# A fused two-block kernel: another order of the 32-, 64- and 128-slot positions in its first mixture of experts

## The chip, the cores and the metric

The kernel runs on one core of a Trainium2 chip. The metric is the device time of one execution in microseconds, the median of several runs. The engines that matter here are TensorE (PE, with its weight loads PEld), VectorE (DVE), ScalarE (ACT), GpSimdE (POOL) and SyncE (SP), whose queue issues nearly all transfers from HBM.

## The reference, cut to what matters

Two transformer blocks are computed for 256 tokens of width 1024, in fp32. The change concerns the first mixture of experts, which sits in the middle of the first block:

```python
logits = hf @ w_router + b_router           # 256 tokens, 32 experts
top_v, top_e = lax.top_k(logits, 4)         # 4 experts for each token
gates = jax.nn.softmax(top_v, axis=-1)
# for each expert e, over the tokens that chose it:
hc = xi @ w1[e] + b1[e]                     # w1[e]: 1024 x 2048
g, u = hc[:, :1024], hc[:, 1024:]
g, u = jnp.minimum(g, 7.0), jnp.clip(u, -7.0, 7.0)
hm = (u + 1.0) * (g * jax.nn.sigmoid(1.702 * g))
yb = hm @ w2[e] + b2[e]                     # w2[e]: 1024 x 1024
# y[token] += gate * yb
```

Each expert's weights are 12 MB of fp32 (8 MB for `w1`, 4 MB for `w2`) and 384 MB for all 32.

## The kernel before

The mixture runs through 32 *positions*, one expert each. A position has a fixed size: 32 slots ("s"), 64 ("m") or 128 ("b", done as two chunks of 64). A slot holds one token. Positions 0 and 1 always hold experts 0 and 1; at run time the other experts are ranked by how many tokens they have, and the ranks are dealt to positions so that larger experts get larger positions (`RANK1`). There are 2 b, 16 m and 14 s. Tokens beyond a position's slots would go to a loop after the positions; with these inputs that loop makes no pass.

For every position the kernel does, in this order:

1. **Loads.** Twelve transfers of 1 MB on SP's queue: eight of `w1` (`in_wei`) and four of `w2` (`in_weo`). From position 2 on SP first reads the expert's number from `oi` (L1106).
2. **First product** (L956 for s, L962 for m and b): for each of the eight `w1` tiles, products of the gathered tokens `xg` with the tile, accumulated in PSUM tiles `h`. An s packs four 32-column products side by side, an m or b two 64-column ones.
3. **Activation**: `h` is copied to `hs` (L973), turned by TensorE (L976), and DVE and ACT make `hm` of it (L979 to L985).
4. **Second product** (L997): `hm` with the four `w2` tiles into PSUM tiles `s`.
5. **Scatter**: `ys` and its two halves (L1010 to L1012), the slot mask (L1005, L1007), products with the mask (L1027), and the sum into `xres` (L1030). It runs beside the next position.

Tokens are gathered for groups of positions with up to 128 slots together (L1050 and L910), ahead of their use. After position 8 the kernel adds the second biases and counts the extra chunks once (L935, L943, L833 to L842).

All weights go through a ring of 17 tiles of 1 MB, `turn % 17`. A load can be issued once the last product that read the tile 17 loads earlier is done. SP's queue is strictly in order, and so is TensorE's; which position's products follow which on TensorE is set when the program is built, by a planner with costs of its own, so two neighbouring positions can be interleaved. The lines on which the change acts:

```python
RING1 = "mmrmrmrmrmrmrmrmm"
def ring_tile():
    turn[0] += 1
    if more_ring:
        pool, order = more_ring
        i = turn[0] % len(order)
todo = [(p, c) for p in range(NE1) for c in CHK1[p]]
for p in range(NE1):
    while (p, CHK1[p][-1]) not in ready or ...:
        gather_on(8)
    er = nc.sync.value_load(route.oi[0:1, p:p + 1], min_val=0, max_val=NE1 - 1)
    expert1(w1, w2, [ready[p, c] for c in CHK1[p]], lambda: places(p), ...)
```

Of the kernel before, what the change touches and what calls it, by code (L numbers as in the profile page):

```python
# [24 lines left out]

NE1, CAP1 = 32, 64
FIX1 = 2
SIZE1 = "mm" + "smsmsbsmsmmsmsmsmsbsmsmmsmsmms"
ROOM1 = [{"b": 128, "m": 64, "s": 32}[c] for c in SIZE1]
CHK1 = [[(o, min(CAP1, r)) for o in range(0, r, CAP1)] for r in ROOM1]  # L30
RANK1 = list(range(FIX1)) + [0] * (NE1 - FIX1)
for _r, _p in enumerate(sorted(range(FIX1, NE1), key=lambda p: -ROOM1[p])):
    RANK1[_p] = FIX1 + _r
assert len(SIZE1) == NE1

# [1837 lines left out]
```

## Time and profile before

| | |
|---|---|
| median of 3 runs | 2324.02 us (2322.54 to 2326.08) |
| the profiled execution | 2327.09 us, span 2325.3 us |
| PE busy | 2158.1 us, 93% of the span |
| DVE busy | 1126.3 us, 48% |
| ACT busy | 785.4 us, 34% |
| mean DMA rate over the span | 300 GB/s |

Busy shares are averages over stages with different limits; the mixture with the 32 positions takes from about 250 to 1235 us of the span. Times in the rows below are microseconds from the start of the span; GB/s is what the core's sixteen DMA engines moved.

### The profile page before, as it was taken

What the parts mean: (1) busy time and instruction counts of PE and PEld (TensorE: products, weight loads), DVE (VectorE), ACT (ScalarE), POOL (GpSimd) and SP (SyncE); (2) the same over time, 40 slices, a digit from 0 to 9 for tenths busy, and PEclk for the clock granted to TensorE, in tenths of its full rate; (3) what the DMA queues carried; (4) which work ended last, traced back from release to release, by engine and by line L of the source; (5) the groups of instructions that cost most, each with busy time, mean ns of one, the idle gap of its engine ahead of it and who ended that gap; (6) DMA issues with size and microseconds to landing.
All of it is one profiled execution on the core that took longest, in us unless ns stands there. A gap on an engine that the chain in (4) does not pass through costs nothing. (4 is left out here: it accounts for less than half of the span.)

```text
span 2325.3 us, 34078 instructions
## 1 busy us (share of the span) xinstructions
PE 2158.1 (93%) x13530; PEld 1424.9 (61%) x13530; DVE 1126.3 (48%) x2048; ACT 785.4 (34%) x1313; POOL 34.9 (2%) x45
## 2 busy tenths in 40 slices
PE   6999999899999889998797999999999899999996
PEld 4888533333333333333235988998888788777983
DVE  3976222323322322322236657654665775337883
ACT  3354211101111111111104655444465564335771
POOL 0000000000000000000000010000001000000000
PEclk9999899998999989999897999999999989999998
DMA  9757689998999999999898334555533467779884
GB/s 395 282 217 271 242 321 417 416 407 344 410 416 416 416 416 412 415 415 416 367 416 335 134 109 164 182 189 183 188 130 110 166 223 275 281 298 349 330 329 197
DMA packets 122630, 697.52 MB, mean 300 GB/s; under 512 B 11120, under 2 KB 11648, under 8 KB 63936
## 3 DMA queue, kind: packets, MB, share of 16 engines
q1 hardware_dynamic: 121120, 690.54, 76.1%
q0 software_dynamic: 1344, 4.73, 0.7%
q8 instruction: 109, 1.79, 0.3%
q14 instruction: 57, 0.47, 0.1%
HBM read 694.18 MB, written 1.05 MB: 299 GB/s over the span
## 5 line engine op out<-in xcount | busy, mean ns | idle before, releaser
L328 DVE TENSOR_TENSOR wl<-w,wh 128x1024 fp32r<-128x1024 f32 (+1 forms) x393 | 476.9, 1223 | 256.7 <-ACT wh L325 247.5
L325 ACT CAST wh<-w 128x1024 fp32r<-128x1024 f32 (+1 forms) x393 | 407.4, 1044 | 304.5 <-PE acc L306 65.7
L962 PE MATMUL h<-w,xg 128*64 128x512 f32 x1280 | 302.0, 620 | 0.0
L997 PE MATMUL s<-w,hm 128*64 128x512 f32 (+1 forms) x1088 | 252.1, 651 | 17.6 <-DVE hm L985 14.1
L962 PEld LDWEIGHTS h<-w,xg 128*64 128x64 f32 x1280 | 93.7, 142 | 186.7 <-issue 182.2
L306 PE MATMUL acc<-xTl,wh 128*128 128x256 f32 x528 | 149.7, 284 | 0.0
L305 PE MATMUL acc<-xTh,wh 128*128 128x256 f32 x528 | 149.7, 283 | 0.0
L307 PE MATMUL acc<-xTh,wl 128*128 128x256 f32 x528 | 149.6, 283 | 0.0
L973 ACT COPY hs<-h 128x512 f32<-128x512 f32 x34 | 19.9, 585 | 373.2 <-PE h L962 290.5
L997 PEld LDWEIGHTS s<-w,hm 128*64 128x64 f32 (+1 forms) x1088 | 62.2, 132 | 130.8 <-issue 95.0
L956 PE MATMUL h<-w,xg 128*32 128x512 f32 x896 | 114.4, 635 | 17.6 <-DMA w<-in_wei 17.6
L973 DVE COPY hs<-h 128x512 f32<-128x512 f32 x20 | 13.8, 691 | 235.9 <-PE h L962 235.9
L910 PEld LDWEIGHTS t<-oh,xh 128*128 128x128 f32 x512 | 70.5, 209 | 76.2 <-ACT xg L911 32.2
L911 ACT ACTIVATE xg<-t,modc,a 128x128 f32<-128x128 f32 (+3 forms) x128 | 55.4, 440 | 182.2 <-PE t L910 126.4
L307 PEld LDWEIGHTS acc<-xTh,wl 128*128 128x128 f32 x528 | 99.3, 188 | 4.2 <-issue 3.1
L305 PEld LDWEIGHTS acc<-xTh,wh 128*128 128x128 f32 x528 | 99.3, 188 | 2.5 <-issue 1.5
L306 PEld LDWEIGHTS acc<-xTl,wh 128*128 128x128 f32 x528 | 99.3, 188 | 2.0 <-issue 1.1
L306 PE MATMUL f<-fxl,wh 128*128 128x256 f32 x352 | 99.9, 284 | 0.0
L305 PE MATMUL f<-fxh,wh 128*128 128x256 f32 x352 | 98.9, 282 | 0.7 <-ACT fxh L1236 0.7
L307 PE MATMUL f<-fxh,wl 128*128 128x256 f32 x352 | 99.3, 283 | 0.0
L910 PE MATMUL t<-oh,xh 128*128 128x128 f32 (+3 forms) x512 | 85.5, 309 | 14.2 <-ACT xg L911 7.1
L1011 ACT CAST ysh<-ys 128x512 fp32r<-128x512 f32 x34 | 21.0, 618 | 222.6 <-DVE ys L1010 207.4
(540 smaller groups left out, 4294.8 us busy)
## 6 DMA issues: line engine op xcount, KB each, us to landing
w<-in_wei SPq DMA_DIRECT2D x256, 1024.0 KB, 18.4
w<-in_weo SPq DMA_DIRECT2D x128, 1024.0 KB, 19.9
w<-in_wm SPq DMA_DIRECT2D x128, 1024.0 KB, 5.8
w<-in_wf SPq DMA_DIRECT2D x33, 1024.0 KB, 4.8
w<-in_w2in SPq DMA_DIRECT2D x32, 1024.0 KB, 5.1
w<-in_wada SPq DMA_DIRECT2D x24, 1024.0 KB, 9.7
w<-in_win SPq DMA_DIRECT2D x16, 1024.0 KB, 8.6
w<-in_w2out SPq DMA_DIRECT2D x8, 1024.0 KB, 4.9
```

The source lines that it names most:

```text
L305: T.matmul(o, l[0], r[0], start=start, stop=False)
L306: T.matmul(o, l[0], r[1], start=False, stop=False)
L307: return T.matmul(o, l[1], r[0], start=False, stop=stop)
L325: A.copy(wh[:, :m], w[:, o:o + m])
L328: V.tensor_sub(wl[:, :m], w[:, o:o + m], wh[:, :m])
L910: T.matmul(pt[:, 0:n], xh2[:, tt, k * P:(k + 1) * P], oh[:, tt, 0:n], start=tt == 0, stop=tt == 1)
L911: taken.append(A.activation(xg[:, k, 0:n], pt[:, 0:n], AF.Identity, bias=sh2[:, k:k + 1], scale=a2[:, k:k + 1]))
L956: T.matmul(ph[0][0][32 * q:32 * q + 32, :].rearrange("p (i c) -> p i c", i=4), chunks[0][:, k], w5[:, q % 2, q // 2], start=k == 0, stop=k ...
L962: T.matmul(p[j][64 * gu:64 * gu + 64, :], xs[:, k], w[:, gu * D + j * 512:gu * D + j * 512 + 512], start=k == 0, stop=k == 7)
L973: (A.copy if j == 0 else V.tensor_copy)(hs[:, j], p[j])
L997: T.matmul(p[r, :], hm[:, kk * 2 + k], w[:, k * D + hf * 512:k * D + hf * 512 + 512], start=kk == 0 and (small or k == 0), stop=kk == 3 an ...
L1011: A.copy(yp[0], ys)
```

## The change

One string is written in another order; nothing else differs. The first two positions stay "mm".

```diff
-SIZE1 = "mm" + "smsmsbsmsmmsmsmsmsbsmsmmsmsmms"
+SIZE1 = "mm" + "ssssmbssmmsmmsmbsssmmmsmmsmmms"
```

Both strings hold the same letters: 14 s, 14 m and 2 b. Position 7 is a b in both; the second b moves from position 20 to 17. The rest of the table (`ROOM1`, `CHK1`, `RANK1`) follows from the string. There are 16 gather groups before and after, and SP issues the same number of loads in the same sequence of ring tiles.

The first difference is on DVE, in the masks `oh` by which the first groups are gathered (`oh_2689` is the group that begins with position 1, `oh_2853` and `oh_2855` the one after it):

```order
 L1050 TENSOR_SCALAR oh_2689<-ca,posm_2601 128x64 x2
-L1050 TENSOR_SCALAR oh_2689<-ca,posm_2601 128x32 x2
-L1050 TENSOR_SCALAR oh_2853<-ca,posm_2601 128x64 x2
-L1050 TENSOR_SCALAR oh_2853<-ca,posm_2601 128x32 x2
+L1050 TENSOR_SCALAR oh_2689<-ca,posm_2601 128x32 x4
+L1050 TENSOR_SCALAR oh_2855<-ca,posm_2601 128x32 x4
+L1050 TENSOR_SCALAR oh_2855<-ca,posm_2601 128x64 x2
```

The first group was position 1 (64) and 2 (32) and is now 1, 2 and 3; the next was 3 (64) and 4 (32) and is now 4, 5 (32 each) and 6 (64).

On TensorE, the end of position 8's second product (an s in both) and the start of position 9's first one. Before (`h_4142` and `h_4143` belong to position 9):

```order
L943 MATMUL t_4107<-beo,gT 128x512
L997 MATMUL s_4056<-w_4075,hm_4005 32x512 x4
L833 MATMUL t_4110<-cnt_2542,perm_2541 32x1
L1027 MATMUL s_4220<-ysh_4087,gt_4084 128x512
L841 MATMUL t_4119<-ca,more_4113 128x32
L842 MATMUL t_4119<-ca,more_4113 128x32
L1027 MATMUL s_4228<-ysh_4087,gt_4084 128x512
L962 MATMUL h_4142<-w_4144,xg_3825 64x512 x2
L962 MATMUL h_4143<-w_4144,xg_3825 64x512 x2
```

Of the change, at the same place (`h_4111` belongs to position 9):

```order
L997 MATMUL s_4025<-w_4044,hm_3980 32x512 x4
L943 MATMUL t_4076<-beo,gT 128x512
L833 MATMUL t_4079<-cnt_2542,perm_2541 32x1
L1027 MATMUL s_4176<-ysh_4056,gt_4053 128x512
L1027 MATMUL s_4184<-ysh_4056,gt_4053 128x512
L1027 MATMUL s_4176<-ysl_4057,gt_4053 128x512
L956 MATMUL h_4111<-w_4112,xg_3438 32x512 x4
L1027 MATMUL s_4184<-ysl_4057,gt_4053 128x512
L841 MATMUL t_4088<-ca,more_4082 128x32
```

The work that is done once after position 8 stays in its place; what follows it is an s now, and was an m.

On TensorE again, positions 27 (m) and 28 (s) of before. `h_6992` and `h_6993` are position 27's first product, `h_7147` position 28's, and `hs_7042` is position 27's copy that the activation starts from. The rows are the last two of position 27's first product, the last four of position 28's, and what follows:

```order
L962 MATMUL h_6992<-w_7036,xg_6320 64x512 x2
L962 MATMUL h_6993<-w_7036,xg_6320 64x512 x2
...
L956 MATMUL h_7147<-w_7172,xg_6320 32x512 x4
L956 MATMUL h_7147<-w_7178,xg_6320 32x512 x4
L956 MATMUL h_7147<-w_7184,xg_6320 32x512 x4
L956 MATMUL h_7147<-w_7190,xg_6320 32x512 x4
L910 MATMUL t_6939<-oh_6927,xh_2417 128x32 x2
L910 MATMUL t_6943<-oh_6927,xh_2417 128x32 x2
L1005 MATMUL t_6972<-cz,posm_2601 128x128 x2
L976 MATMUL t_7047<-cz,hs_7042 128x128 x4
```

Of the change, positions 27 (s, second product into `s_7073`) and 28 (m, first product into `h_7118` and `h_7119`, copy `hs_7168`):

```order
L997 MATMUL s_7073<-w_7086,hm_7024 32x512 x4
L997 MATMUL s_7073<-w_7092,hm_7024 32x512 x4
L962 MATMUL h_7118<-w_7120,xg_6448 64x512 x2
L962 MATMUL h_7119<-w_7120,xg_6448 64x512 x2
...
L962 MATMUL h_7118<-w_7162,xg_6448 64x512 x2
L962 MATMUL h_7119<-w_7162,xg_6448 64x512 x2
L910 MATMUL t_7065<-oh_7053,xh_2417 128x32 x2
L910 MATMUL t_7069<-oh_7053,xh_2417 128x32 x2
L1005 MATMUL t_7098<-cz,posm_2601 128x128 x2
L976 MATMUL t_7173<-cz,hs_7168 128x128 x4
```

Before, the whole first product of position 28 stood between position 27's first product and the turning of its result, so position 27's second product came after both. In the changed program no position stands between the first and the second product of another; a position's first product does stand directly behind the second product of the one before, ahead of the gather, mask and scatter work of that one, at 5 to 6, 9 to 10, 11 to 12, 13 to 14, 15 to 16, 19 to 20, 21 to 22, 23 to 24, 25 to 26 and 27 to 28. Before, that was so at 14 to 15, 16 to 17, 18 to 19, 22 to 23, 24 to 25 and 26 to 27.

## Rows read from the trace of the kernel before

**Rows 1.** The page: GB/s in 40 slices of the span, each 58 us.

```profile
GB/s 395 282 217 271 242 321 417 416 407 344 410 416 416 416 416 412 415 415 416 367 416 335 134 109 164 182 189 183 188 130 110 166 223 275 281 298 349 330 329 197
```

**Rows 2.** Windows of the mixture; the last column is the DMA rate.

```profile
core 0: us, PE busy (x) PEld busy (x) DVE busy (x) ACT busy (x) POOL busy (x), PEclk, DMA share, GB/s
340.00:367.00 27.00, 24.07 (x144) 9.50 (x144) 8.96 (x19) 3.35 (x7) 0.00 (x0) 0.87 1.01 400
367.00:516.00 149.00, 136.55 (x706) 51.52 (x703) 41.75 (x94) 18.87 (x40) 0.00 (x0) 0.98 1.02 415
516.00:605.00 89.00, 82.67 (x420) 31.01 (x416) 28.96 (x65) 11.20 (x23) 0.00 (x0) 0.92 0.92 361
605.00:1138.00 533.00, 476.02 (x2406) 178.37 (x2406) 148.05 (x318) 63.24 (x135) 0.00 (x0) 0.93 1.01 415
1110.00:1117.00 7.00, 5.32 (x28) 0.61 (x24) 0.00 (x0) 0.00 (x0) 0.00 (x0) 0.50 1.02 422
1138.00:1160.00 22.00, 21.64 (x120) 8.62 (x122) 8.14 (x15) 3.16 (x7) 0.00 (x0) 1.00 0.73 300
367.00:1235.00 868.00, 783.05 (x3964) 291.91 (x3960) 249.82 (x538) 101.41 (x215) 0.00 (x0) 0.94 1.00 406
```

**Rows 3.** The page: DMA issues, with the median us to landing.

```profile
w<-in_wei SPq DMA_DIRECT2D x256, 1024.0 KB, 18.4
w<-in_weo SPq DMA_DIRECT2D x128, 1024.0 KB, 19.9
w<-in_wf SPq DMA_DIRECT2D x33, 1024.0 KB, 4.8
```

**Rows 4.** Timeline of SP: first issue and length, positions 5, 7, 7, 8, 20, 29.

```profile
378.40 22.60 SPq L247 DMA_DIRECT2D w<-in_wei  x8
...
437.62 17.94 SPq L247 DMA_DIRECT2D w<-in_wei  x8
457.73 10.18 SPq L247 DMA_DIRECT2D w<-in_weo  x4
...
468.75 17.27 SPq L247 DMA_DIRECT2D w<-in_wei  x8
...
864.42 9.76 SPq L247 DMA_DIRECT2D w<-in_weo  x4
...
1118.54 29.94 SPq L247 DMA_DIRECT2D w<-in_wei  x8
```

**Rows 5.** Timeline of PE at positions 2, 7, 7, 8, 9, 10, 11, 12, 20, 31.

```profile
340.28 1.06 PE L956 MATMUL h<-w,xg 128*32 128x512 f32 x8
...
471.03 27.69 PE L962 MATMUL h<-w,xg 128*64 128x512 f32 x128
...
513.63 10.51 PE L997 MATMUL s<-w,hm 128*64 128x512 f32 x44
...
524.71 1.90 PE L956 MATMUL h<-w,xg 128*32 128x512 f32 x10
...
559.23 3.68 PE L962 MATMUL h<-w,xg 128*64 128x512 f32 x8
...
594.84 1.06 PE L956 MATMUL h<-w,xg 128*32 128x512 f32 x8
...
616.90 13.95 PE L962 MATMUL h<-w,xg 128*64 128x512 f32 x64
...
647.70 1.94 PE L962 MATMUL h<-w,xg 128*64 128x512 f32 x8
...
917.07 10.51 PE L997 MATMUL s<-w,hm 128*64 128x512 f32 x44
...
1222.30 1.06 PE L956 MATMUL h<-w,xg 128*32 128x512 f32 x8 [1.27 <-DMA w<-in_wei]
```

**Rows 6.** Timeline of PE where position 28's first product and 27's second begin.

```profile
1108.42 1.94 PE L956 MATMUL h<-w,xg 128*32 128x512 f32 x8 [7.01 <-DMA w<-in_wei]
...
1134.46 1.12 PE L997 MATMUL s<-w,hm 128*64 128x512 f32 x2 [1.74 <-DVE xres L1030]
```

## The prediction

> **What bounds the kernel now.** I read the DMA rate over the whole span first, then windows of the mixture, then the order of time on SP and on TensorE. The page's GB/s line stands at 407 to 416 from the seventh slice on and stays there until the mixture ends, with dips to 344 and 367 [rows 1]. Everywhere else it is far lower. So the mixture's loads run at a ceiling of 416 GB/s, and one load of 1 MB takes 1048576 B / 416 GB/s = 2.52 us, the twelve of a position 30.2 us. Summed over 367 to 1235 us the rate is 406 [rows 2]: the loads lost 868 x (1 - 406/416) = 20.9 us against the ceiling. Two windows hold nearly all of it: 516 to 605 with 361 GB/s, 89 x (1 - 361/416) = 11.8 us, and 1138 to 1160 with 300, 22 x (1 - 300/416) = 6.1 us, together 17.9; the 533 us between them ran at 415 and lost 1.3 [rows 2]. TensorE had work that is as long: from the starts of positions 7, 8, 10, 11 and 12 on PE, a b takes 524.71 - 471.03 = 53.7 us, an s 616.90 - 594.84 = 22.1, an m 647.70 - 616.90 = 30.8 [rows 5]. So an s gives back 8.1 us against the loads, an m loses 0.6, a b loses 23.5. At the end of the mixture it is the loads that TensorE waits for: the last tile of position 31's first product came after a wait of 1.27 us on DMA [rows 5]. What moves the last load therefore moves the end, and what TensorE wins by itself does not.
>
> **When the DMA engines run dry.** A ring tile is loaded again 17 loads later, at full rate 17 x 2.52 = 42.8 us after its own issue. With the queue full a load lands 18.4 to 19.9 us after its issue, an undisturbed one after 4.8 [rows 3], so the reissue can be some 15 us late before the engines are empty. A tile must thus be read within about 42.8 + 15 = 57.8 us of its issue; I call the time from issue to last reading its age. Two places test this. Position 7, the first b, issued its four `w2` loads from 457.73 on, the last at about 465.3 (three loads of 2.52 later) [rows 4], and read the last tile until 513.63 + 10.51 = 524.1 [rows 5]: age 58.8, over the limit, and the rate falls from 516 on [rows 2]. The second b, position 20, issued its last at 864.42 + 7.6 = 872.0 [rows 4] and read it until 917.07 + 10.51 = 927.6 [rows 5]: age 55.6, under the limit, and there the window shows no loss [rows 2]. The first loss grew after the b: position 8 took 559.23 - 524.71 = 34.5 us instead of 22.1 [rows 5], since the second biases and the count of extra chunks are done there, and an m followed it while the ring was already full. The other loss has another cause. Position 28's first product had to wait 7.01 us for its first tile at 1108.42 and was paced by its loads, and position 27's second product, which stood behind it in TensorE's order, began at 1134.46 [rows 6]; so four tiles of position 27 were held, and SP needed 29.94 us for position 29's eight loads where 17.27 to 22.60 stand at positions 5, 7 and 8 [rows 4].
>
> **The change, part by part.** No instruction's work is removed: 14 s, 14 m and 2 b after the first two, as before, and the same loads. A few gather products become 128 columns wide where they were 96 or 64; by 13.95 us for 64 rows of 512 columns [rows 5] 32 more columns on 16 products cost 16 x 0.22 x 32/512 = 0.06 us, hidden or not: nothing.
>
> *Start.* The loads of positions 3 and 4 wait for tiles of positions 1, 2 and the first of 3; positions 1 and 2 are an m and an s in both programs. The rate is at 400 from 340 and at 415 from 367 [rows 2]. So the four small ones win no load there; I take 0, bounded by what 340 to 367 lacks, 27 x (1 - 400/416) = 1.0 us.
>
> *Four s ahead of the first b.* TensorE begins position 2 at 340.28 [rows 5]. With s, s, s it begins position 5 at 340.28 + 3 x 22.1 = 406.6, 28.2 us after that position's first issue at 378.40 [rows 4]; position 6 at 428.7, 20.1 after its issue (378.40 + 30.2 = 408.6), which is the time to land: TensorE has caught up. The m at 6 is then paced by its loads. Its eighth tile lands at 408.6 + 7 x 2.52 + 20 = 446.2, and what an m does from there is 30.8 - 13.95 + 1.7 = 18.6 us, so the b at 7 begins at 464.8 instead of 471.03. Its last tile is read by 464.8 + 53.1 = 517.9 (53.1 is 524.1 - 471.03), age 52.6, 5.2 under the limit. The gather and mask work that now stands behind position 6's first product may cost up to these 5 us; then the b starts as before and only its own share of the loss comes back.
>
> *s, s behind the first b.* Position 8 keeps its extra work, which I take at the same 34.5 us; position 9 then begins at 464.8 + 53.7 + 34.5 = 553.0 instead of 559.23, and is an s. Its first load is issued at 468.75 + 30.2 = 499.0 [rows 4], age 54. Position 10 begins at 575.1, 46 us after its issue; before it was 594.84 [rows 5]. So the 11.8 us come back.
>
> *The second b at 17.* Between lie positions 10 to 16, five m and two s: 5 x 30.8 + 2 x 22.1 = 198.2 us against 7 x 30.2 = 211.4 of loads. The distance to the issue falls from 46 to 32.8 us. The b's last tile has then the age 32.8 + 53.1 - 11 x 2.52 = 58.2: 0.4 over. If position 7 had begun 5 us later it would be 5 over. I take 1.9 us of new loss here, between 0 and 6. Behind it three s bring the distance from 56 to 32, and eight m and two s from there to about 20.5 at position 31, so TensorE ends on the last loads as before.
>
> *27 to 28.* In the changed order no first product stands between the two products of another position, so the 6.1 us come back. The single interleavings, of which there are more, stood at five places between 605 and 1080 and cost nothing there: that window's rate is 415 [rows 2].
>
> Sum: 11.8 + 6.1 - 1.9 = 16.0 us. The profiled execution took 2327.09 us, its span 2325.3, so about 1.8 lie around it; it is 3.1 above the median of the runs, 2324.02, and I carry the difference over: span 2309.3, profiled 2311.1, **median 2308.0**. Behind the mixture nothing is moved.
>
> **The rivals.** Less than 0.2%, 4.65 us, a measurement of this kernel could hardly tell from no change.
>
> 1. *The loss moves to the second b.* If position 7 starts no earlier and TensorE is 5 to 6 us later throughout, some 2 us remain at 7 and 8 and 6 at 17: gain 17.9 - 8 = 10, time 2314. For it: the computed margin at 17 is nothing. Against: 20 had a margin with a shorter run of s behind it.
>
> 2. *No change.* If TensorE stands 13 us later at 17 than I work out (slow tiles behind the mass of interleaved first products), the b there loses 13.4 or more beyond the 0.4, and 2322 to 2325 results.
>
> 3. *Slower by the clock.* When TensorE has caught up it waits for tiles. After the 7.01 us wait eight rows of an s took 1.94 us [rows 6] where they took 1.06 elsewhere [rows 5], and 1110 to 1117 shows a granted clock of 0.50 [rows 2], the 1.2 GHz level, against 2.4. An m at that level would need 13.95 x (1.94 - 1.06)/1.06 = 11.6 us more for its first product and by the same ratio some 8.7 more for its second (10.5 us): 51 us against 30.2 of loads. Positions 28 to 30 are three m behind a caught-up s. One at the low level wholly gives 2308 + 20 = 2328, two give 2348; it decides from 16 us on. The Trainium skill, "TensorE: Matmul & The Clock Gate", section "HAM oscillation — how this bites in real kernels", describes this: matmuls that wait for each tile of a DMA start cold every time. By that rule the runs of small positions, which make TensorE wait, would be paid for in the m behind them. Rows agree with it at 1108. Against a full m at the low level speaks that such stretches, wherever they lay, were short enough to leave a mean clock of 0.93 between 605 and 1138 [rows 2], and that they lie in tiles that are waited for anyway.
>
> 4. *More.* The 1.3 us of 605 to 1138, the 1.0 of 340 to 367 and no new loss at 17 give 17.9 + 2.3 and, with scatter, 2302 to 2303.
>
> **How the numbers follow.** The forecast, loads nearly unbroken from 367 on and 12 to 20 us gained, has 0.62; rival 1 has 0.16, rival 4 0.09, rival 2 0.07, rival 3 0.06. The range 2301 to 2317 holds the forecast, rivals 1 and 4: 0.87 on paper, and I leave a part of this for periods taken from single positions. Faster 0.87, same 0.07, slower 0.06.
>
> **What would show it.** After: 405 GB/s or more in every window from 516 to 605; position 7 beginning near 465 and 9 near 553; SP issuing eight `w1` loads in 17 to 23 us at every position between 5 and 31 but one or two behind a b; the end of the last first product near 1207 instead of 1223, still behind a wait on DMA. The start (to 367) unchanged within 1 us. Wrong: a window of 300 to 360 GB/s behind position 17, rival 1 or 2; PE rows at the 1.94 us pace in positions 28 to 30 with the loads held back, rival 3.

## The result, and the profile after

The changed kernel takes 2306.96 us, the median of 6 runs (2302.28 to 2309.73), against 2322.64 for the kernel before, 6 runs beside them (2319.93 to 2326.08): the ratio is 0.9931, with a 95% interval of 0.9918 to 0.9943, so 15.7 us less. The forecast was 16.0 less and 2308.0. The profiled execution has a span of 2306.7 us, 18.6 under that of before, where 16 was forecast; single executions of either kernel differ by several us, so the two numbers do not contradict each other.

The page's GB/s line of the changed kernel, in 40 slices of 57.7 us, answers to [rows 1]:

```profile
GB/s 395 287 206 270 238 346 416 416 409 405 416 416 417 416 415 416 416 415 416 416 416 284 136 105 152 201 188 187 185 117 126 155 243 256 283 314 349 324 334 195
```

The two dips, 344 and 367, are 405 and 416 now, and the stretch at the ceiling ends earlier: the 22nd slice has 284 where it had 335. The windows of the changed kernel (columns as in [rows 2]: the last is the DMA rate, the one two before it the granted clock):

```profile
250.00:367.00 117.00, 108.99 (x568) 48.65 (x572) 34.38 (x95) 22.35 (x49) 0.30 (x1) 0.93 0.89 334
367.00:516.00 149.00, 130.60 (x684) 48.98 (x677) 39.03 (x86) 18.47 (x39) 0.00 (x0) 0.95 1.02 415
516.00:720.00 204.00, 190.89 (x975) 73.69 (x972) 66.91 (x147) 26.31 (x56) 0.00 (x0) 0.94 1.01 412
720.00:1130.00 410.00, 371.03 (x1912) 140.32 (x1914) 117.69 (x249) 50.19 (x109) 0.00 (x0) 0.95 1.02 416
1100.00:1180.00 80.00, 71.80 (x322) 26.55 (x322) 21.14 (x42) 7.42 (x17) 0.00 (x0) 0.98 1.02 416
```

and three of the same windows in the trace of before, so that the losses can be counted alike in all kernels:

```profile
250.00:367.00 117.00, 108.79 (x525) 48.46 (x526) 33.10 (x87) 20.73 (x47) 0.00 (x0) 0.88 0.87 322
...
516.00:720.00 204.00, 187.83 (x937) 70.97 (x933) 60.60 (x133) 25.44 (x53) 0.00 (x0) 0.94 0.98 392
...
1100.00:1180.00 80.00, 64.07 (x310) 21.50 (x308) 22.77 (x47) 7.90 (x18) 0.00 (x0) 0.85 0.93 381
```

Against a ceiling of 416 the window 516 to 720, the *hole behind the first b*, lost 204 x (1 - 392/416) = 11.8 us before and loses 2.0 now. The window 1100 to 1180, the *crossing* of positions 27 and 28, lost 80 x (1 - 381/416) = 6.7 us and loses nothing. That is 16.5 us. The start, 250 to 367, moved 12 GB/s more, worth 117 x 12/416 = 3.4 us; the experiments below bear on how much of this belongs to the change.

The landings of the loads are a second way to count. Where nothing holds them, the twelve loads of a position land in 30.2 us; a stretch of positions that takes longer has lost the rest. In the trace of before the mixture's last load lands at 1232.5 us, in that of the change at 1213.9, which is 18.6 us earlier. Up to position 8's last load the change is 2.2 us ahead. From there to position 13's last load before loses 12.2 us and the change 2.3, and from position 27's to position 31's before loses 5.7 and the change 0.3; the remaining 1.2 us are spread between. For one hole the two counts differ by up to 3 us. Below, "by landings" means this count over the same two stretches.

TensorE of the changed kernel at positions 7, 8, 9 and 31 (start, length, line, tiles; in brackets the idle time before and what ended it) answers to [rows 5]:

```profile
465.12 27.69 PE L962 MATMUL h<-w,xg 128*64 128x512 f32 x128
...
509.99 10.51 PE L997 MATMUL s<-w,hm 128*64 128x512 f32 x44
...
521.08 1.90 PE L956 MATMUL h<-w,xg 128*32 128x512 f32 x10
...
549.88 1.93 PE L956 MATMUL h<-w,xg 128*32 128x512 f32 x8
...
1203.73 1.94 PE L956 MATMUL h<-w,xg 128*32 128x512 f32 x8 [0.58 <-DMA w<-in_wei]
...
1211.67 6.54 PE L997 MATMUL s<-w,hm 128*32 128x512 f32 x32 [0.91 <-DVE hm L985]
```

The first b begins at 465.12 (464.8 was forecast, 471.03 before). SP of the changed kernel (first issue, length, count), positions 7, 7, 9 and 10:

```profile
435.92 17.93 SPq L247 DMA_DIRECT2D w<-in_wei  x8
456.01 10.17 SPq L247 DMA_DIRECT2D w<-in_weo  x4
...
496.28 30.94 SPq L247 DMA_DIRECT2D w<-in_wei  x8
...
531.53 25.96 SPq L247 DMA_DIRECT2D w<-in_wei  x8
```

The b's last tile was issued at about 456.01 + 7.6 = 463.6 and read by 520.5: age 56.9, against 58.8 before and the estimated limit of 57.8. SP still issues late for positions 9 and 10 (31 and 26 us for eight loads), but the rate fell by little, to 412 over 516 to 720. The last first product of the mixture ends at 1205.7 instead of 1223.4, again behind a wait on DMA.

### The profile page after: what moved, and what is told of

Read it like the earlier page. It is cut to its first block, busy times and chain, and to the rows that moved or that the text cites. A ratio compares the mean times of both kernels' runs of the same rounds, so it can differ in the third digit from the quotient of the medians.

```text
span 2306.7 us, 34090 instructions
## 1 busy us (share of the span) xinstructions
PE 2143.9 (93%) x13530; PEld 1420.7 (62%) x13530; DVE 1125.6 (49%) x2048; ACT 785.1 (34%) x1313; POOL 34.9 (2%) x45
## 5 line engine op out<-in xcount | busy, mean ns | idle before, releaser
L962 PE MATMUL h<-w,xg 128*64 128x512 f32 x1280 | 294.7, 602 | 9.3 <-DMA w<-in_wei 9.3
L1010 DVE TENSOR_TENSOR ys<-s,g2s 128x512 f32<-128x512 f32 x34 | 23.5, 691 | 161.3 <-PE s L997 161.2
```

Of the source, the lines that this page charges most:

```text
L962: T.matmul(p[j][64 * gu:64 * gu + 64, :], xs[:, k], w[:, gu * D + j * 512:gu * D + j * 512 + 512], start=k == 0, stop=k == 7)
L1010: V.tensor_tensor(ys, p, g2s, op=ALU.mult)
```

## The experiments

Times below are medians of each kernel's runs and of before's runs beside them; ratios carry a 95% interval, and a gain in us is the ratio's unless the medians are named. All orders hold the same letters.

**Only the tail of the new order.**

```diff
-SIZE1 = "mm" + "smsmsbsmsmmsmsmsmsbsmsmmsmsmms"
+SIZE1 = "mm" + "smsmsbsmsmmsmsmsmsbsmssmmsmmms"
```

> Positions 2 to 23 as before, 24 to 31 as in the change (s m m s m m m s). No first product stands between the two products of another position any more; the front is untouched. Theory (two separate holes in the loads): only the 6.1 us of 1138 to 1160 come back, 2324 - 6 = about 2317 where before runs at 2323, and the window 516 to 605 stays near 361 GB/s. Rival (only the order around the first b counts): no change, within 3 us of before. Rival (TensorE is what ends the mixture): no change either, since its work is the same.

2317.76 us against 2322.89, ratio 0.9977 (0.9966 to 0.9988): 5.3 us less (5.1 by the medians). Its windows:

```profile
516.00:720.00 204.00, 187.91 (x941) 71.38 (x941) 59.95 (x131) 25.60 (x54) 0.00 (x0) 0.95 0.99 395
...
1100.00:1180.00 80.00, 71.88 (x326) 26.58 (x326) 25.71 (x51) 6.94 (x15) 0.00 (x0) 0.95 1.02 417
```

The first hole stands nearly as before (10.3 us), the crossing's is gone, and the time is what the second is worth (5.5 us by landings). The two holes are separate, and both rivals that expected no change fall.

**Two small ones behind the first b, the front as before.**

```diff
-SIZE1 = "mm" + "smsmsbsmsmmsmsmsmsbsmsmmsmsmms"
+SIZE1 = "mm" + "smsmsbssmmmsmsmsmsbsmsmmsmsmms"
```

> Before with positions 9 and 10 exchanged (s, m instead of m, s): two small ones behind the first b, nothing else; the crossing at 27 and 28 stays. Theory: the b at 7 starts as before (471), so what is lost while position 8 runs (some 2 us at position 9's loads, some 4 at 10's) stays, and the rest of the first hole, 5 to 6 us, goes: 5 us faster than before, 3 to 8. Rival (only what stands ahead of the b counts): no change.

2320.91 us against 2322.89, ratio 0.9987 (0.9977 to 0.9997): 3.0 us less, and 2.0 by the medians: at the lower edge of the expected 3 to 8, or under it. Its windows:

```profile
250.00:367.00 117.00, 108.80 (x539) 49.12 (x540) 33.09 (x87) 21.02 (x48) 0.00 (x0) 0.91 0.88 331
...
516.00:720.00 204.00, 187.49 (x938) 71.31 (x934) 62.82 (x139) 26.05 (x55) 0.00 (x0) 0.95 1.00 402
...
1100.00:1180.00 80.00, 66.82 (x308) 23.53 (x308) 22.48 (x47) 7.32 (x17) 0.00 (x0) 0.84 0.88 358
```

The first hole shrinks from 11.8 to 6.9 us, as the theory has it. But the window of the crossing now loses 11.2 us instead of 6.7: its first product stands in TensorE's order wherever TensorE is, and what was won ahead of it is spent waiting there (11.05 us for the first tile, 7.01 before). By landings the first hole gives 4.4 us and the crossing takes 4.4 back.

**One more small one ahead of the first b, one fewer behind it.**

```diff
-SIZE1 = "mm" + "smsmsbsmsmmsmsmsmsbsmsmmsmsmms"
+SIZE1 = "mm" + "sssmsbsmmmmsmsmsmsbsmsmmsmsmms"
```

> Before with positions 3 (m) and 10 (s) exchanged: one more small one ahead of the first b, one fewer behind it; the crossing at 27 and 28 stays. Theory: the b at 7 starts some 6 us earlier, near 465, its last tile is under the limit of 57.8 us, and though three m follow position 8 their ages stay near 55: 9 us faster than before, 6 to 12. Rival (small ones behind the b are what counts): slower by 3 or more, since m follows m there.

2318.38 us against 2322.89, ratio 0.9977 (0.9965 to 0.9988): 5.3 us less. One statement of the expectation was wrong: the planner laid this program out without the crossing, so 6.7 us came from there. Its windows:

```profile
516.00:720.00 204.00, 186.71 (x857) 69.41 (x858) 59.78 (x129) 22.52 (x48) 0.00 (x0) 0.91 0.97 381
...
1100.00:1180.00 80.00, 73.10 (x362) 27.16 (x358) 21.67 (x45) 8.00 (x19) 0.00 (x0) 0.93 1.02 417
```

The hole behind the b did not close; it grew to 17.2 us. The b did begin early, at 463.54, and its last tile had an age of 53.1, 4.7 under the estimated limit. But position 8 again took 34.6 us, and of the four m behind it (the expectation counted three) the first two held tiles for 59 to 60 us where 55 was expected. So the theory failed on this hole and the rival was right: what follows the b matters as much as what precedes it, and the age of the b's last tile alone does not tell whether loads are lost.

**The new order up to position 23, the old tail.**

```diff
-SIZE1 = "mm" + "ssssmbssmmsmmsmbsssmmmsmmsmmms"
+SIZE1 = "mm" + "ssssmbssmmsmmsmbsssmmmmmsmsmms"
```

> Positions 2 to 23 as in the change, 24 to 31 as before (m m s m s m m s). No crossing stands in this program either. Theory: both holes are gone as in the change, 16 us faster than before, 12 to 20, and within 3 of the change. Rival (the tail's order has a worth of its own, without the crossing): 10 us faster only.

2304.92 us against 2322.89, ratio 0.9926 (0.9907 to 0.9944). This is the change's time within its interval. The old tail is harmless once nothing crosses in it; no worth of the tail's order itself shows.

**The second b close behind the first.**

```diff
-SIZE1 = "mm" + "ssssmbssmmsmmsmbsssmmmsmmsmmms"
+SIZE1 = "mm" + "ssssmbssbmsmmsmmsssmmmsmmsmmms"
```

> The change with positions 10 (m) and 17 (b) exchanged: the second b comes three positions behind the first. No crossing. Theory of the age limit: position 10 starts some 43 us after its first issue (before the b had 33), so its last tile has an age of 43 + 53 - 28 = 68 us, 10 over the limit of 57.8: the loads lose 8 to 12 us there and none at 17, so about 10 slower than the change, 6 faster than before. Rival (any order with runs of small ones and no crossing will do): as the change.

2333.66 us against 2323.14, ratio 1.0037 (1.0024 to 1.0051) to before: 26 us slower than the change where 10 was expected. The rival falls, and the size of the theory is off. Its windows:

```profile
516.00:720.00 204.00, 193.32 (x917) 73.28 (x917) 62.90 (x139) 23.66 (x50) 0.00 (x0) 0.88 0.88 352
720.00:1130.00 410.00, 366.18 (x1848) 139.62 (x1847) 113.57 (x240) 48.49 (x103) 0.00 (x0) 0.93 1.02 416
```

SP of the same kernel, the eight `w1` loads of positions 10 and 12 (start, length):

```profile
527.40 32.20 SPq L247 DMA_DIRECT2D w<-in_wei  x8
...
606.17 40.29 SPq L247 DMA_DIRECT2D w<-in_wei  x8
```

And its TensorE, where positions 10, 11 and 12 begin:

```profile
575.61 26.82 PE L962 MATMUL h<-w,xg 128*64 128x512 f32 x122
...
637.73 1.93 PE L962 MATMUL h<-w,xg 128*64 128x512 f32 x6
...
669.89 2.78 PE L956 MATMUL h<-w,xg 128*32 128x512 f32 x24
```

204 x (1 - 352/416) = 31.4 us are lost in the first window and none in the second. The b at 10 began 575.6 - 527.4 = 48 us after its issue, not 43, and took 637.7 - 575.6 = 62.1 us, not 53.7, with a granted clock of 0.88 over the window. The m behind it, 32 us, kept the lateness up before an s gave the first of it back. That a b which begins this late loses loads is confirmed (its last tile had an age of 73.5), but the expected 8 to 12 us were far too few: my sum stopped at the b itself, and the m behind it still held tiles for up to 76.5 us.

**Less TensorE work, in the change and in before.** Half of the scatter's products are left out, in both kernels by the same edit.

```diff
-                for y in yp:
-                    for hf in range(2):
-                        r = slice(64 * hf, 64 * hf + 64)
-                        T.matmul(po[hf], gt[r, tt * P:(tt + 1) * P], y[r, :], start=y is yp[0], stop=y is yp[1])
+                for hf in range(2):
+                    r = slice(64 * hf, 64 * hf + 64)
+                    T.matmul(po[hf], gt[r, tt * P:(tt + 1) * P], yp[0][r, :], start=True, stop=True)
```

> The change with the low halves of ys left out of the scatter's products (half of L1027's matmuls; this part of the sum is missing in the output): some 1.5 us of TensorE time less for each of the 34 chunks, 50 us in all. Theory (the loads end the mixture): the same time as the change within 4 us, TensorE only waits longer for tiles. Rival (TensorE ends it): faster than the change by 20 us or more. Rival (the clock falls when TensorE waits): slower than the change.

2310.13 us against 2323.14, ratio 0.9946 (0.9933 to 0.9960): not faster than the change, and 3.2 us slower by the medians. The window of the whole mixture in the thinned change (PE busy first, granted clock third from the end):

```profile
250.00:1222.00 972.00, 866.87 (x4351) 330.14 (x4352) 280.95 (x625) 121.88 (x262) 0.00 (x0) 0.92 0.99 402
```

and the same window in the change:

```profile
250.00:1222.00 972.00, 880.79 (x4502) 338.12 (x4502) 284.63 (x630) 123.50 (x265) 0.30 (x1) 0.94 1.00 404
```

The busy time fell by 13.9 us and not by 50; the change's trace has such products side by side (two begin at 522.91, two at 523.25), and the clock fell from 0.94 to 0.92. So the test is weaker than meant. It is also not clean, since the page of the thinned change shows a new dip:

```profile
GB/s 397 286 216 270 230 357 416 416 416 394 416 416 416 416 370 415 417 415 415 416 416 329 134 109 148 201 185 185 191 117 128 155 241 256 283 314 350 323 334 195
```

The 15th slice, 807 to 864 us, has 370 where the change has 415. It stands behind the second b, which began 34.0 us after its first issue here (29.1 in the change) and whose last tile had an age of 62.0 (55.5): this is the loss that the forecast's first rival expected at the second b. The granted clock over 605 to 740 was 0.91, against 0.99 in the change; that this made the b late is likely and not shown. By landings 6 us are lost there, so the mixture's last load lands 4.5 us later than in the change, while the span behind that load is 6.6 us shorter, in part because this edit shortens the scatter that ends the mixture. So less TensorE work did not make the mixture shorter, as the theory has it, but the equal times of the two kernels are a sum of a loss and a gain.

The same edit in before:

> Before with the same half of L1027's matmuls left out. Theory: the b at 7 starts some 7 us earlier because TensorE is faster, so the first hole (11.8 us) closes without any change of order, while the crossing at 27 and 28 keeps its 6 us: 12 us faster than before, 9 to 15. Rival (TensorE ends the mixture): 40 us faster or more. Rival (the order itself, not the lateness of TensorE, makes the hole): no change.

2312.73 us against 2323.14, ratio 0.9952 (0.9939 to 0.9966): 11 us less, the size expected, by another route than expected. Its windows:

```profile
516.00:720.00 204.00, 183.09 (x906) 70.79 (x904) 62.22 (x140) 25.61 (x54) 0.00 (x0) 0.92 1.00 405
...
1100.00:1180.00 80.00, 68.38 (x298) 24.90 (x292) 24.63 (x50) 7.93 (x18) 0.00 (x0) 0.79 0.85 346
```

The first hole fell to 5.4 us without a change of order, so TensorE's lateness has the larger part in it; it did not close, although the b's last tile had an age of only 53.1. The crossing's grew to 13.5, which takes that back in the mixture (6.3 us won and 6.6 lost by landings). The mixture's last load landed 4.8 us earlier than in before, about what it was ahead at the start; the other 5.6 us of the two spans' difference lie behind that load, where this edit shortens the last scatter too.

**A ring of 16 tiles, in the change and in before.**

```diff
-RING1 = "mmrmrmrmrmrmrmrmm"
-PRE1 = 4
+RING1 = "mrmrmrmrmrmrmrmm"
+PRE1 = 3
```

> The change with a ring of 16 tiles instead of 17 (and three instead of four tiles loaded ahead for position 1). Theory: the age limit falls by 2.5 us to about 55.3. The change's b at 7 has a last tile of age 57.0 in its trace, that at 17 55.5, so 2 us are lost at these and up to 3 at the start: 2 to 5 us slower than the change. Rival (the ring's depth has no part): the same as the change.

2310.90 us against 2323.14, ratio 0.9952 (0.9939 to 0.9966): 3.9 us above the change's median, as expected. By landings 1.9 us of this stand behind the first b, where some were expected, and none at the second b or at the start up to position 8.

The same edit in before:

> Before with a ring of 16 tiles instead of 17 (and three instead of four tiles loaded ahead for position 1), the counterpart of the same cut in the change, which made that 4 us slower. Theory: the first hole grows by the 2.5 us of one tile at least, the b at 20 comes to its limit (55.6 against 55.3), and 1 to 3 us go at the start: 4 to 8 us slower than before. Rival: no change.

2331.77 us against 2323.29, ratio 1.0044 (1.0032 to 1.0056): 8.5 by the medians, 10 by the ratio, a little more than expected. By landings the first hole grows by 2.2 us, as expected, and the crossing by 3.4, which was not; at the second b nothing is lost, where its limit was expected. The profiled execution is only 3.4 us over that of before, so the traces do not place all of the 8 to 10 us. Both edits also load one tile fewer ahead, so depth and start are not separated by the times alone. The new order needs the 17th tile less than the old one: it costs 4 us there and 8 to 10 here. A ring deeper than 17 was not tried.

**The extra work after position 8 moved to a later small position, in before and in the change.**

```diff
-            if p == 8:
+            if p == 13:
```

> Before, with the second biases and the count of extra chunks done after position 13 (an s) instead of 8; the order of sizes as before, the crossing at 27 and 28 stays. Theory (the hole behind the first b comes from its lateness plus the 12 us of extra time in position 8): position 8 takes about 23 us, position 9 begins near 548 instead of 559, the hole shrinks from 11.9 to 1 to 4 us, the crossing keeps 6 to 10: 6 to 10 us faster than before. Rival (the b's own lateness and the m behind it make the hole): 0 to 3 us faster.

2314.31 us against 2323.29, ratio 0.9966 (0.9953 to 0.9979): 8 us less, as expected. Its windows:

```profile
516.00:720.00 204.00, 187.27 (x945) 71.91 (x942) 64.26 (x142) 26.21 (x55) 0.00 (x0) 0.96 1.01 412
...
1100.00:1180.00 80.00, 68.97 (x326) 25.07 (x320) 24.93 (x50) 7.93 (x18) 0.00 (x0) 0.86 0.89 363
```

Its positions 8 and 9 on TensorE begin here:

```profile
523.85 1.90 PE L956 MATMUL h<-w,xg 128*32 128x512 f32 x10
...
551.51 13.95 PE L962 MATMUL h<-w,xg 128*64 128x512 f32 x64
```

With the sizes in their old order the first hole is as small as the change makes it (2.0 us; 3.7 by landings, for 2.3); position 8 takes 551.51 - 523.85 = 27.7 us (about 23 was expected). The crossing's grew again, to 10.2 (7.3 by landings, 5.7 before). The b was as late as before: its last tile had an age of 59.1, over the estimated limit, and only these 2 us were lost. So the hole was the sum of a b that came late, of extra work directly behind it, and of an m behind that. Taking away the extra work alone closed it down to these 2 us; an earlier b alone (the thinned before) left 5.4 us and an s for the m alone left 6.9.

In the change the same work went to position 12:

```diff
-            if p == 8:
+            if p == 12:
```

> The change, with that same work done after position 12 (an s) instead of 8. Theory: the 1.8 us that the change still loses at position 9 go and nothing else can, since the loads are then unbroken from position 4 on: 0 to 3 us faster than the change, not to be told from it. Rival (the work after position 8 costs time of its own wherever the loads stand): 10 us faster than the change.

2307.39 us against 2323.29, ratio 0.9939 (0.9926 to 0.9952): the change's time. The 1.8 us that were expected to go did not: 516 to 720 runs at 413 GB/s for 412, and by landings 2.1 us are lost there for 2.3. So what is left behind the first b has mostly another cause than the extra work, and that cause is open.

No version was clearly faster than the change; the new order with the old tail (ratio 0.9926) cannot be told from it.

## Why the prediction was right

**The bound and the two holes** (right). That the loads bound the mixture, that two interruptions cost 11.8 and 6.1 us, and that the new order removes both is what the windows show (2.0 and 0 left), and the tail alone was worth 5.3 us in runs. Thinning TensorE's work did not make the loads of the change land earlier.

**The age limit** (useful, but not the test that the forecast made of it). The 57.8 us are an estimate, and the forecast applied them to the b's last tile. Over all runs that one age does not order the losses: 53.1 went with 17.2 and 5.4 us lost, 56.9 with 2.0, 58.8 with 11.8 and 59.1 with 2.0. Where much was lost, tiles of the positions behind the b were held for about 60 us as well (64 in before, 60 in the two with 53.1, at most 58 behind the b in the run with 59.1).

**The first b earlier, two s behind it** (right, with two errors that offset each other). Position 7 began at 465.12 for 464.8. I had the b's last tile at age 52.6; it was 56.9. Of the 4.3 us, 1.7 come from its loads, which were issued that much earlier (456.01 against 457.73), and 2.4 from the activation and scatter work between its two products, 492.8 to 498.65 us against 498.7 to 502.2 before; the later start is the rest. That is inside the 5 us that the text allowed for. Position 9 still began early, at 549.88 for 553.0, since position 8 took 28.8 us where I had kept 34.5. Two s behind an old front left 6.9 us of hole, and the earlier b of the thinned before 5.4, so neither half alone does it; the run with three s ahead and four m behind (17.2) is no clean test of the first half, as it also took an s away behind the b.

**The second b at 17** (wrong in place, harmless). I took 1.9 us of loss there; the rate from 720 to 1130 is 416, none. It began 29.1 us after its first issue for 32.8, and its last tile had an age of 55.5 for 58.2. SP was late for position 19 behind it (29.4 us for eight loads), and the rate did not fall. The 2.0 us that are left stand behind position 7 instead. The steps' errors cancelled in the sum, so that 15.7 was measured for 16.0 is in part luck: the terms are off by up to 2 us each, and the start and the end, which the sum has at nothing, brought some 2 to 3 and cost 2.4.

**The start** (taken as 0 and forecast as unchanged within 1 us, measured as 3.4 by the rate and 2.2 by landings, and partly open). The five programs that begin "mmsss" and have all their work and 17 tiles ran at 332 to 338 GB/s there, the four with the old front and 17 tiles at 319 to 331. The one at 331 has exactly the front of before up to position 8, so a good part of the difference is scatter; why the rest arises was not tried.

**The end.** The mixture's last product ended at 1211.67 + 6.54 = 1218.2, 16.2 us earlier than the 1234.4 of before. The last load landed 18.6 us earlier, so 2.4 us were lost again at position 31: there TensorE waited for its tiles, ran its last first product at the slow pace (1.94 us for eight rows where 1.06 is usual), and its second product took 6.54 us for 5.98 before. The granted clock was 0.80 over 1192 to 1206 and 0.56 over 1206 to 1219, where before it was 1.00 over 1214 to 1224 and 0.69 over 1224 to 1235. The 2.4 us that the span moved beyond 16.2 lie behind the mixture, where nothing was changed, and the medians of the runs (15.7) do not show them.

**A slip.** The wider gather products come to 16 x 0.22 x 32/512 = 0.22 us and not 0.06; they are nothing either way.

**The rivals.** The clock: the granted clock over 1100 to 1180 is 0.98, so the m at 28 to 30 did not fall to the low level for long. The waits for tiles were there. The cold start behind such a wait that the Trainium skill, "TensorE: Matmul & The Clock Gate", section "HAM oscillation — how this bites in real kernels", describes shows in the time of the change at position 31 alone, with the 2.4 us above. The loss that moves to the second b did not come, because 17 follows a stretch in which TensorE had caught up; it did come in the thinned change, where that b stood 34.0 us behind its first issue, and the run with that b at 10 shows it at its worst.

## What to carry to other kernels

Where a stream of loads is the bound and a ring holds them, look for the places where the DMA rate leaves its ceiling, and ask which tiles were read too late: the age that a tile may have is about the ring's depth times the time of a load plus the slack of the queue, and all tiles behind a large piece have to be looked at, not its last one alone. In this kernel the order of large and small pieces mattered by the worst lateness that it made, until small pieces followed, and not by its mean; the small pieces had to stand on both sides of a large one. Work that is done once, and can be done anywhere, should not stand behind a large piece: moving it gave the old order half of the whole gain, and the new order nothing. And read the engine's order as the planner left it: one product put ahead of its turn cost about half of what the large hole did, and its price grew when other waits were removed.

## What was not expected of the hardware

Making TensorE earlier made the crossing dearer: 6.7 us before, 10.2 to 13.5 in the three programs that removed part of the first hole and kept the crossing (by landings 5.7, and 7.3 to 12.3). A late b can cost far more than its own lateness: 31.4 us were lost behind one that began 48 us after its issue, with an m behind it, where the kernel before began its first b 33 us after [rows 4, 5] and lost 11.8. And half of the scatter's products less left TensorE's busy time only 13.9 us lower over the mixture, at a granted clock of 0.92 instead of 0.94.
